# GpSimd makes the low part of every second half tile in the first stretch of the expert products

## The chip, the cores and the metric

The kernel runs on one core of a Trainium2 chip. The core has five engines that run side by side, each with its own queue of instructions taken in order: TensorE (PE in the profile, its weight loads PEld) multiplies matrices, VectorE (DVE) and ScalarE (ACT) work element by element, GpSimd (POOL) does element work too, and SyncE (SP) issues most transfers. [...] The metric is the device time of one execution in microseconds (us).

## The reference, cut to what matters

One decoder block for 256 tokens of width 2048: a projection, two kinds of attention, a gated merge, a layer norm, and then a retrieval over 16384 experts of one neuron each. The change lies in the last part, which reads, cut:

```python
def chunk(yc):                              # 128 tokens
    q = (yc @ w_q).reshape(PEER_CHUNK, PEER_HEADS, 2, half)
    s1 = einsum('chd,nd->chn', q[:, :, 0], sub_k1)
    s2 = einsum('chd,nd->chn', q[:, :, 1], sub_k2)
    v1, i1 = lax.top_k(s1, 16)
    v2, i2 = lax.top_k(s2, 16)
    ...
    sc, j = lax.top_k(cand, 16)             # of the sums v1 + v2
    eid = take_along_axis(cid, j, axis=-1)  # which experts
    gate = softmax(sc)
    act = gelu(einsum('chkd,cd->chk', u_tab[eid], yc))
    return einsum('chk,chkd->cd', gate * act, v_tab[eid])
```

The kernel multiplies the tokens with all rows of `u` and all rows of `v`, and brings in the choice of experts through tables of gates that are zero where an expert is not chosen.

## The kernel before, in words

Every float32 product is made of three passes in TensorE's float32r format. A weight tile `raw` is split into a high part `hi` (a cast) and a low part `lo = raw - hi`; the token matrix is split in the same way (`yhi`, `ylo`), and the passes are hi x yhi, lo x yhi and hi x ylo.

`Stream` (L56 to L130) does the splitting for all weights. A job is one weight tile of 128 x 1024 floats. `load_to` issues its transfer on SP's queue into one of three `raw` buffers; `split_upto` then treats the tile as two half tiles of 512 columns (b = 0 and b = 1): ScalarE makes `hi` of the half (L98), and VectorE makes `lo` of it (L99). There are six buffers each for `hi` and `lo`, so three tiles. The flag `share` sends `lo` of the half b = 1 to GpSimd in place of VectorE; it is set in a part of the attention and cleared later, and is off in the expert part.

`step` (L146) is the unit of the program. It takes the next split tile, runs what was deferred, takes at most one piece of background work from a list of `slots` when enough credit has gathered (each step gives a credit of 1, each piece has a cost), then calls `W.ahead()`, which writes the splits of the tiles up to two ahead into the queues, and last the matmuls of its own tile. So VectorE's and GpSimd's queues hold, for each step: the instructions of a background piece, if there is one, and behind them the `lo` of the tile that is used two steps later.

In the expert part, each of the 64 products `p` takes four steps of 24 matmuls (8 blocks of 128 x 128, three passes each), of which the second already needs `lo` of half 0 and the fifth `lo` of half 1. ScalarE applies GELU to the finished sum (L1251, `G<-acc`). While these products run, the background pieces choose the experts, in this order: `key_top` (the best 16 of 128 keys, 16 pieces of cost 1.7, on VectorE; half of them come before and half after a second batch of scores), and then for each of two tiles of 128 tokens t: `cands`, four `cand_top`, eight `pick` (cost 1.4), `gate` and `sel_T`. After those comes the piece that calls `open_G(1)` (it opens the second gate table and makes `keys` on GpSimd), and then 65 pieces that fill the gate tables.

A `pick` of head h is a small chain over two engines:

```python
V.tensor_tensor(eq, iota[...], posf[...], op=OP.is_equal)        # L1107, VectorE
GP.tensor_tensor(eq, eq, cid[...], op=OP.mult)                   # L1109, GpSimd
if (t, h - 1) in eqs:
    V.tensor_reduce(out=eid[:, t, h - 1, :], in_=eqs.pop((t, h - 1)), ...)   # L1111, VectorE
```

Before the expert part, `h_rows` (L1036, L1037) scales and shifts the normalised rows on GpSimd in 16 instructions of 128 x 512, and stores them.

Of the kernel before, what the change touches and what calls it, by code (L numbers as in the profile page):

```python
# [130 lines left out]
def block_kernel(ctx, tc, x, xT, w_in, rel_bias, onehot, lamq, lamk, subln_g, pe, w1, w2k, w2v, cmask,  # L131
# [11 lines left out]
    W = Stream(nc, stream, 3, 6)  # L143
# [40 lines left out]
    def bg(cost, pre, post=None):  # L184
        slots.append((cost, pre, post))
# [845 lines left out]
    def h_rows():  # L1031
        for t in range(2):
            for n in range(4):
                c = slice(n * 512, n * 512 + 512)
                d = r1[:, t, c]
                GP.tensor_tensor(d, d, gb[:, 0, c], op=OP.mult)  # L1036
                GP.tensor_tensor(d, d, gb[:, 1, c], op=OP.add)  # L1037
            GP.dma_start(h_d[:, t, :], r1[:, t, :])
# [112 lines left out]
    def open_G(i):  # L1151
        if i == 0:
            h_rows()
            pL.close()
        else:
            pT.close()
            gs["oh"] = pO.enter_context(tc.tile_pool(name="ohp", bufs=1, side="right"))
            gs["n0"] = len(stashed)
            keys = gs["keys"] = gs["oh"].tile([128, 128, 2], F16, name="keys")
            GP.iota(keys, pattern=[[1, 128], [0, 2]], base=0, channel_multiplier=0,  # L1160
                    allow_small_or_imprecise_dtypes=True)
        gp = pG[i].enter_context(tc.tile_pool(name=f"gp{i}", bufs=1))
        gs["G", i] = gp.tile([128, HI, S], F32, name=f"G{i}")
# [62 lines left out]
                pO.close()  # L1226
        deferred.append(ev)

    bg(0.1, lambda: open_G(1))
    for q in range(65):  # L1230
        bg(GCOST, lambda q=q: g_onehot(q) if q < 64 else None, lambda q=q: g_mm(q - 1) if q else None)

# [271 lines left out]
```

## Time and profile before

| | before |
|---|---|
| median of 3 runs | 2222.72 us (2221.65 to 2224.61) |
| the profiled execution | 2224.97 us |
| its span in the trace | 2223.2 us |
| PE busy | 2184.4 us, 98% |
| DVE busy | 1452.2 us, 65% |
| ACT busy | 1130.3 us, 51% |
| POOL busy | 246.5 us, 11% |

The time of the profiled execution is 1.8 us longer than its span, which runs from the first to the last instruction. Busy shares are averages over the whole span; the stretch that the change touches, from 765 to 970 us of the span, has other shares. TensorE's granted clock is full in all slices of it. A row of the trace gives where an instruction starts and how long it took; for an element engine an instruction that follows another on the same engine starts while the one before drains, so the distance between two starts (some 0.08 us less than the duration) is what a row of like instructions costs. An instruction that its engine has begun but that cannot get at its data shows as a longer duration and not as idle time.

### The profile page before, as it was taken

Reading aid. Unit: us, or ns where it says so; the run is one execution under the profiler, and the core shown is the slowest. Engines: PE = TensorE matmul, PEld = TensorE weight load, DVE = VectorE, ACT = ScalarE, POOL = GpSimd, SP = SyncE. Lnnn points to the kernel's source line nnn. Section 1 sums busy time; section 2 is a strip of 40 time slices with the busy share of each in tenths; the row PEclk is TensorE's granted clock in tenths of the full one; section 3 lists DMA queues with packets and bytes.
Section 4 is the critical chain, followed back from the end, with each engine's and each line's share of the span. In section 5 each row is a group of like instructions: output and inputs, shape, how many; then the busy total and the mean of one; then the engine's idle time right before and its main releaser. Section 6 shows DMA issues by size and latency. Waiting matters only on the chain.

```text
span 2223.2 us, 40705 instructions
## 1 busy us (share of the span) xinstructions
PE 2184.4 (98%) x15712; PEld 2016.0 (91%) x15712; DVE 1452.2 (65%) x2898; ACT 1130.3 (51%) x2153; POOL 246.5 (11%) x223
## 2 busy tenths in 40 slices
PE   9999999999999999999999999999999999999997
PEld 9988999999987999999999999998888888888786
DVE  5558774665767889988886555555555555555567
ACT  5555654665545444455554444445555455554443
POOL 2002234443001501210000000000000000000002
PEclk9999999999999999999999999999999999999999
DMA  7664564545675766555656666666666666667774
GB/s 243 195 186 155 173 198 130 166 151 162 202 226 160 238 183 189 181 185 181 182 183 190 196 194 194 193 197 206 196 191 194 193 193 196 192 197 236 253 220 143
DMA packets 119843, 424.72 MB, mean 191 GB/s; under 512 B 13876, under 2 KB 14212, under 8 KB 119392
## 3 DMA queue, kind: packets, MB, share of 16 engines
q1 hardware_dynamic: 111600, 398.90, 58.0%
q0 software_dynamic: 5600, 18.75, 2.8%
q10 hardware_dynamic: 2448, 4.46, 0.5%
q8 instruction: 123, 2.02, 0.4%
q14 instruction: 72, 0.59, 0.1%
HBM read 413.37 MB, written 8.69 MB: 190 GB/s over the span
## 4 chain that ended last, share of the span: by engine, by line
PE 75%; DVE 8%; DMA 5%; ACT 2%; issue 2%; POOL 1%; ACTq 0%; DVEq 0%; POOLq 0%; SPq 0%
PE acc L191 43%; PE o L191 27%; DVE lo L99 4%; PE lg L191 2%; DMA raw<-in_v_dram 2%; DMA raw<-in_w_in_dram 1%; PE pv L191 1%; DMA raw<-in_wout_dram 1%; DMA raw<-in_wq_dram 1%; ACT hi L98 1%; PE tp L539 1%; DVE eq L1107 0%; DVE eid L1111 0%; DVE st L901 0%; DVE r L933 0%
## 5 line engine op out<-in xcount | busy, mean ns | idle before, releaser
L99 DVE TENSOR_TENSOR lo<-raw,hi 128x512 fp32r<-128x512 f32 (+1 forms) x1422 | 980.8, 719 | 551.2 <-ACT hi L98 549.2
L98 ACT CAST hi<-raw 128x512 fp32r<-128x512 f32 (+1 forms) x1494 | 872.4, 617 | 692.5 <-PE o L191 267.6
L191 PE MATMUL acc<-yhi,lo 128*128 128x256 f32 x2112 | 586.7, 278 | 5.5 <-DVE lo L99 5.5
L191 PE MATMUL acc<-yhi,hi 128*128 128x256 f32 x2112 | 591.4, 280 | 0.0
L191 PE MATMUL acc<-ylo,hi 128*128 128x256 f32 x2112 | 584.1, 277 | 0.0
L191 PEld LDWEIGHTS acc<-yhi,lo 128*128 128x128 f32 x2112 | 397.0, 188 | 9.4 <-DVE lo L99 9.1
L191 PEld LDWEIGHTS acc<-yhi,hi 128*128 128x128 f32 x2112 | 396.8, 188 | 0.4 <-ACT hi L98 0.2
L191 PEld LDWEIGHTS acc<-ylo,hi 128*128 128x128 f32 x2112 | 396.7, 188 | 0.0
L191 PE MATMUL o<-lo,whi 128*128 128x512 f32 x1000 | 389.7, 390 | 0.8 <-DVE lo L99 0.8
L191 PE MATMUL o<-hi,whi 128*128 128x512 f32 x1000 | 389.4, 389 | 0.6 <-ACT hi L98 0.5
L191 PE MATMUL o<-hi,wlo 128*128 128x512 f32 x1000 | 389.1, 389 | 0.0
L191 PE MATMUL acc<-xhi,hi 128*128 128x256 f32 x1024 | 290.7, 284 | 4.2 <-ACT hi L98 4.2
L191 PE MATMUL acc<-xhi,lo 128*128 128x256 f32 x1024 | 286.5, 280 | 5.5 <-DVE lo L99 5.3
L191 PE MATMUL acc<-xlo,hi 128*128 128x256 f32 x1024 | 285.2, 279 | 0.0
L191 PEld LDWEIGHTS o<-lo,whi 128*128 128x128 f32 x1000 | 187.7, 188 | 42.0 <-DVE lo L99 3.1
L191 PEld LDWEIGHTS o<-hi,whi 128*128 128x128 f32 x1000 | 187.7, 188 | 40.9 <-ACT hi L98 1.5
L191 PEld LDWEIGHTS o<-hi,wlo 128*128 128x128 f32 x1000 | 187.7, 188 | 38.5
L191 PEld LDWEIGHTS acc<-xhi,lo 128*128 128x128 f32 x1024 | 194.1, 190 | 7.8 <-DVE lo L99 7.7
L191 PEld LDWEIGHTS acc<-xhi,hi 128*128 128x128 f32 x1024 | 194.4, 190 | 6.0 <-ACT hi L98 5.6
L191 PEld LDWEIGHTS acc<-xlo,hi 128*128 128x128 f32 x1024 | 193.9, 189 | 0.0
L1282 POOL DMA_DIRECT2D back<-act_d x17 | 9.3, 546 | 1170.5 <-DVE G L1290 607.4
L99 POOL TENSOR_TENSOR lo<-raw,hi 128x512 fp32r<-128x512 f32 x72 | 104.1, 1450 | 231.7 <-ACT hi L98 228.0
(308 smaller groups left out, 2170.3 us busy)
## 6 DMA issues: line engine op xcount, KB each, us to landing
raw<-in_u_dram SPq DMA_DIRECT2D x256, 512.0 KB, 4.1
raw<-in_v_dram SPq DMA_DIRECT2D x256, 512.0 KB, 3.6
raw<-in_w_in_dram SPq DMA_DIRECT2D x143, 512.0 KB, 4.1
raw<-in_wout_dram SPq DMA_DIRECT2D x32, 512.0 KB, 4.2
raw<-in_wbda_dram SPq DMA_DIRECT2D x16, 512.0 KB, 3.9
raw<-in_wbnsa_dram SPq DMA_DIRECT2D x16, 512.0 KB, 3.8
raw<-in_wq_dram SPq DMA_DIRECT2D x16, 512.0 KB, 4.2
raw<-in_w_in_dram SPq DMA_DIRECT2D x16, 280.0 KB, 3.0
```

Source lines behind the costliest of these rows:

```text
L98: self.nc.scalar.copy(hi[:, :w], r)
L99: (self.nc.gpsimd if self.share and b else sub).tensor_tensor(lo[:, :w], r, hi[:, :w].bitcast(F32), op=OP.subtract)
L191: PE.matmul(o, a, b, start=start, stop=stop, skip_group_check=True)
L539: PE.transpose(tp[:, 128 * b:128 * b + 128], P[:, 128 * b:128 * b + 128], ident)
L1282: GP.dma_start(t, act_d[vorder[n]])
```

## The change

`W.share` is set where the list of background pieces is written, just ahead of the first expert product, and cleared by the piece that opens the second gate table. Between the two, `lo` of the half b = 1 goes to GpSimd's queue.

```diff
+    def unshare():
+        W.share = False
+        open_G(1)
+
+    W.share = True
-    bg(0.1, lambda: open_G(1))
+    bg(0.1, unshare)
```

The instruction that moves is the one of L99, in `split_upto`:

```python
(self.nc.gpsimd if self.share and b else sub).tensor_tensor(lo[:, :w], r, hi[:, :w].bitcast(F32), op=OP.subtract)
```

On VectorE, at the picks of the first token tile (`eq<-iota,posf` is L1107 of a pick, `eid<-eq` the sum of the pick before it, `lo<-raw,hi` the low parts of one or two weight tiles):

```order
 L1107 TENSOR_TENSOR eq<-iota,posf 128x800
-L99 TENSOR_TENSOR lo<-raw,hi 128x512 x4
+L99 TENSOR_TENSOR lo<-raw,hi 128x512 x2
 L1107 TENSOR_TENSOR eq<-iota,posf 128x800
 L1111 TENSOR_REDUCE eid<-eq 128x16
-L99 TENSOR_TENSOR lo<-raw,hi 128x512 x2
+L99 TENSOR_TENSOR lo<-raw,hi 128x512
 L1107 TENSOR_TENSOR eq<-iota,posf 128x800
 L1111 TENSOR_REDUCE eid<-eq 128x16
-L99 TENSOR_TENSOR lo<-raw,hi 128x512 x4
+L99 TENSOR_TENSOR lo<-raw,hi 128x512 x2
 L1107 TENSOR_TENSOR eq<-iota,posf 128x800
```

Between two picks VectorE keeps one `lo` of each weight tile where it had two. Between the eight picks of a token tile lie 2, 1, 2, 1, 1, 2 and 1 weight tiles, so ten.

On GpSimd, from the store at the end of `h_rows` (`h_d<-r`) over the first picks (`eq<-eq,cid` is L1109):

```order
 L1038 DMA h_d<-r_8480 128x2048
-L1109 TENSOR_TENSOR eq<-eq,cid 128x800 x16
+L99 TENSOR_TENSOR lo<-raw,hi 128x512 x36
+L1109 TENSOR_TENSOR eq<-eq,cid 128x800
+L99 TENSOR_TENSOR lo<-raw,hi 128x512 x2
+L1109 TENSOR_TENSOR eq<-eq,cid 128x800
+L99 TENSOR_TENSOR lo<-raw,hi 128x512
+L1109 TENSOR_TENSOR eq<-eq,cid 128x800
```

GpSimd, which had only the 16 products of the picks in this stretch, has 71 low parts among them: 36 ahead of the first pick, 10 between the picks of each token tile, 11 between the two tiles, and 4 at the end, ahead of the making of `keys`. The queues of TensorE, ScalarE and SP keep their order.

## Rows read from the trace of the kernel before

**Rows 1.** The page: busy time of each engine, and VectorE in 40 slices.
```profile
PE 2184.4 (98%) x15712; PEld 2016.0 (91%) x15712; DVE 1452.2 (65%) x2898; ACT 1130.3 (51%) x2153; POOL 246.5 (11%) x223
...
DVE  5558774665767889988886555555555555555567
```

**Rows 2.** Busy time of each engine by stretch of the expert part.
```profile
core 0: us, PE busy (x) PEld busy (x) DVE busy (x) ACT busy (x) POOL busy (x), PEclk, DMA share, GB/s
770.00:865.00 95.00, 95.00 (x821) 94.39 (x821) 84.64 (x381) 46.06 (x81) 0.00 (x0) 1.00 0.64 194
865.00:900.00 35.00, 34.30 (x296) 33.60 (x294) 33.84 (x39) 15.17 (x28) 14.55 (x8) 1.00 0.55 174
...
1200.00:1500.00 300.00, 300.00 (x2650) 300.00 (x2649) 159.18 (x249) 139.09 (x249) 0.00 (x0) 1.00 0.65 194
```

**Rows 3.** Waits of PEld, 770 to 970 us: total us, times, longest.
```profile
PEld acc L191 <- DVE lo L99: 6.6, 15, 1.6
```

**Rows 4.** ScalarE in order of time, 855 to 870 us: start, duration, [idle before].
```profile
854.84 0.60 ACT L1251 ACTIVATE G<-acc 128x512 f32<-128x512 f32 x1 [1.92 <-PE acc L191]
...
865.72 0.60 ACT L1251 ACTIVATE G<-acc 128x512 f32<-128x512 f32 x1 [1.92 <-PE acc L191]
```

**Rows 5.** VectorE in order of time over the picks of the first token tile.
```profile
865.85 0.99 DVE L1107 TENSOR_TENSOR eq<-iota,posf 128x800 f32<-128x800 f32 x1
...
879.90 0.98 DVE L1107 TENSOR_TENSOR eq<-iota,posf 128x800 f32<-128x800 f32 x1
880.80 0.98 DVE L1111 TENSOR_REDUCE eid<-eq 128x16 f32<-128x800 f32 x1
881.70 2.24 DVE L99 TENSOR_TENSOR lo<-raw,hi 128x512 fp32r<-128x512 f32 x2
883.86 0.98 DVE L1107 TENSOR_TENSOR eq<-iota,posf 128x800 f32<-128x800 f32 x1
...
896.95 0.98 DVE L1107 TENSOR_TENSOR eq<-iota,posf 128x800 f32<-128x800 f32 x1
...
899.86 0.99 DVE L1115 TENSOR_REDUCE eid<-eq 128x16 f32<-128x800 f32 x1 [1.04 <-POOL eq L1109]
900.77 2.49 DVE L99 TENSOR_TENSOR lo<-raw,hi 128x512 fp32r<-128x512 f32 x4
```

**Rows 6.** GpSimd in order of time, 865 to 970 us.
```profile
881.03 1.76 POOL L1109 TENSOR_TENSOR eq<-eq,cid 128x800 f32<-128x800 f32 x1 [3.40 <-DVE eq L1107]
...
898.07 1.76 POOL L1109 TENSOR_TENSOR eq<-eq,cid 128x800 f32<-128x800 f32 x1 [2.19 <-DVE eq L1107]
```

**Rows 7.** GpSimd in order of time, `h_rows`.
```profile
739.79 1.74 POOL L1036 TENSOR_TENSOR r<-r,gd 128x512 f32<-128x512 f32 x1
...
743.19 1.74 POOL L1036 TENSOR_TENSOR r<-r,gd 128x512 f32<-128x512 f32 x1
...
746.59 1.73 POOL L1036 TENSOR_TENSOR r<-r,gd 128x512 f32<-128x512 f32 x1
```

**Rows 8.** VectorE in order of time, the same stretch.
```profile
738.95 13.83 DVE L99 TENSOR_TENSOR lo<-raw,hi 128x512 fp32r<-128x512 f32 x8 [1.22 <-ACT hi L98]
```

**Rows 9.** VectorE in order of time, 311 to 320 us (attention, `share` set).
```profile
311.74 2.36 DVE L630 TENSOR_TENSOR r<-r,gsub 128x1024 f32<-128x1024 f32 x1
...
318.65 1.23 DVE L630 TENSOR_TENSOR r<-r,gsub 128x1024 f32<-128x1024 f32 x1
```

**Rows 10.** GpSimd in order of time, 311 to 320 us.
```profile
311.72 1.29 POOL L99 TENSOR_TENSOR lo<-raw,hi 128x512 fp32r<-128x512 f32 x1 [1.09 <-DMA raw<-in_w_in_dram]
```

**Rows 11.** All `lo` on GpSimd: duration in ns, min/median/max.
```profile
L99 POOL TENSOR_TENSOR lo<-raw,hi x72: 1267/1358/1991, 298.1 to 701.9; 128x512 fp32r<-128x512 f32 x72
```

**Rows 12.** VectorE's groups, 770 to 865 us: busy us, mean ns, idle before.
```profile
L99 DVE TENSOR_TENSOR lo<-raw,hi 128x512 fp32r<-128x512 f32 x70 | 44.2, 685 | 10.3 <-ACT hi L98 10.3
```

## The prediction

> **What bounds the kernel now.** I read the page first. TensorE is busy 98% of the span, and VectorE 65%, but VectorE's slices are uneven: from the 14th to the 21st it stands at eight and nine tenths, against five in the last third [rows 1]. A slice is 55.6 us; the stretch of the change is the first half of that hump, so I cut it out. From 770 to 865 us, where the keys are ranked, VectorE is busy 84.64 of 95 us and TensorE the whole 95; from 865 to 900 us, the picks of the first token tile, VectorE is busy 33.84 of 35 and TensorE falls to 34.30; from 1200 to 1500 us TensorE is busy throughout beside a half idle VectorE [rows 2]. So TensorE sets the time nearly everywhere, and what it loses is lost at the end too, since nothing behind the stretch has idle time in which to win it back. The waits of the weight loads say how much there is: from 770 to 970 us they waited for `lo` 15 times, 6.6 us in all, 1.6 us at most [rows 3]. That is the most that a perfect version of this change could win, 0.3% of the time.
>
> The pace that TensorE wants comes from ScalarE's GELUs, one for every four steps: 865.72 - 854.84 = 10.88 us, so 2.72 us a step [rows 4]. At the picks the program asks for more than that. From the first `eq` to the eighth, 896.95 - 865.85 = 31.1 us pass [rows 5], and ten weight tiles are split in them, for which TensorE takes 27.2 us. VectorE is 3.9 us behind there; the tiles split ahead cover a part, and the rest, with the tail behind the eighth pick, are the waits of [rows 3].
>
> **Why VectorE is behind** decides this case. One cycle of a pick with one weight tile runs from 879.90 to 883.86 us, 3.96 us [rows 5]. By the starts of rows, `eq` costs 0.90 and the sum `eid` 0.90. The two `lo` should cost 0.60 each, as the four at 900.77 show (2.49 us: three distances of 0.60 and one duration of 0.69). But here the two take 2.24 us instead of 1.29: the first starts at 881.70, while GpSimd's product of the pick runs from 881.03 to 882.79 [rows 5, 6], and the pair ends 1.15 us behind that product's end, about the time of the two alone. So VectorE's subtraction stood still for 0.95 us until GpSimd was done. The sum `eid`, which reads one tensor, ran beside the same product at its usual 0.98 us. In `h_rows` the same is seen without a break: GpSimd starts an instruction of 128 x 512 twice per 3.40 us (739.79, 743.19, 746.59), so every 1.70 us [rows 7], and beside it eight `lo` take 13.83 us, 1.73 each in place of 0.60 [rows 8]. The two engines take turns. And where GpSimd made a `lo` in the attention part, VectorE's multiplication of two tensors took 2.36 us against 1.23 us a little later without it [rows 9, 10].
>
> [...]
>
> **The change, part by part.**
>
> 1. Removed from VectorE: 71 `lo` at 0.60 us, 43 us of its work. Where VectorE is not what TensorE waits for, this is worth nothing.
>
> 2. Added to GpSimd: the same 71. Alone one takes 1.27 us at the least and 1.36 us in the median [rows 11]. What matters is how long it keeps VectorE from its two-tensor instructions. A turn of both engines costs 1.70 us, of which 0.60 is VectorE's, so 1.10 us [rows 7, 8]; the multiplication that was held up gives 2.36 - 1.23 = 1.13 us [rows 9]. I take 1.10, from the stretch where the turns follow each other without a gap, as they will at the picks.
>
> 3. At the picks VectorE's queue alternates `eq`, `eid`, `lo`, and GpSimd's the product and `lo`. [...] Per weight tile 0.60 us go and 1.10 us come, +0.50 us. The cycle of 3.96 us becomes 4.46, where TensorE wants 2.72. Ten tiles between the first and the eighth pick: 31.1 + 5.0 = 36.1 us, against 27.2.
>
> 4. Two things are given back per token tile. Behind the eighth pick VectorE sums twice (the second from 899.86) and then splits (900.77) [rows 5]; GpSimd's `lo` can now run under the second sum. The second half of that weight tile then needs no 0.60 us behind the first, and GpSimd's turn costs a little of this: -0.4 us. And while keys are ranked, VectorE's other instructions read one tensor each, GpSimd's `lo` runs beside them, and the second half is ready earlier by up to one VectorE `lo`, 0.60 us; the splitting enters the picks with that much more lead: -0.5 us.
>
> 5. From 770 to 865 us VectorE made 70 `lo` in 44.2 us and idled 10.3 us before them [rows 12]; TensorE was busy for all 95 us there, and GpSimd idle [rows 2]. I cost the 35 that move at nothing: their cover is VectorE's idle time and the instructions with one input. What it costs if that cover fails is the third rival.
>
> 6. `W.share = True`, the piece `unshare` and the order on the other engines cost nothing: no instruction is added for them. The last four `lo` on GpSimd stand ahead of `keys`, some 5 us, where GpSimd sat idle in the trace before; if they were late, the first gate piece would start late with them.
>
> Sum: 5.0 - 0.4 - 0.5 = +4.1 us for each of the two token tiles, +8.2 us. On the profiled execution that makes 2224.97 + 8.2 = 2233.2 us; it stood 2.25 us above the median of its runs, so by the median 2222.72 + 8.2 = 2230.9, which I round to 2231.
>
> The bounds of the price: below, GpSimd always has a `lo` waiting and loses no time between VectorE's `eq` and its product (881.03 comes 0.23 us after VectorE's queue was free to go on, at 880.80), which saves seven times 0.23 = 1.6 us a tile, so +2.5 a tile and +5 in all. Above, each `lo` holds VectorE for its median of 1.36 us [rows 11]: +0.76 for ten tiles is 7.6, less 0.9, twice: +13.4 us. The forecast's own range is 2228 to 2236.
>
> **The rivals.**
>
> *Faster: the low parts of the two engines don't exclude each other.* Then the cycle loses 0.60 us a weight tile, 31.1 - 6.0 = 25.1 us, under TensorE's 27.2, and GpSimd's own queue (seven products of 1.76 and ten `lo` of 1.36, 25.9 us) just fits. All 6.6 us of waits would go: 2216 us. For it: the products at the picks are longer than a `lo` and read other tensors. Against it: [rows 7, 8] are a subtraction of just this kind beside a GpSimd instruction of the same size. It decides if a GpSimd `lo` holds VectorE under 0.60 us. 9%.
>
> *About the same.* The lead grows more than I allow, or GpSimd's `lo` falls under `eid` and under waits that exist now (the 0.95 us of [rows 5]), so that the picks cost 0 to 4.4 us in all: about 2225 us. [...] 15%.
>
> *Slower still: the ranking of keys falls behind too.* If every GpSimd `lo` holds VectorE for 1.10 us there as well, VectorE's 84.64 us become 84.64 + 35 x 0.50 = 102.1 us, over the 95 that TensorE gives [rows 2, 12]. The 7 us come in two waves, each covered in part by the lead; at worst all 7 are paid, and the picks begin without lead. +10 to +20 us, about 2238. For it: VectorE would have no idle time left. Against it: most of its work there reads one tensor. 14%.
>
> **The numbers.** Forecast 62% (+5 to +13.4), 14% slower still, 15% about the same, 9% faster. I call a difference under 0.2%, 4.4 us, no change, about what a measurement of this kernel can tell. Slower then has 0.62 + 0.14 = 0.76, same 0.15, faster 0.09. The range reaches to 2224 below, into the case of about the same, and to 2242 above, into the ranking case; it leaves out the faster case, a third of the same and the worst of the ranking, under 2 in 10.
>
> **What the new profile should show.** Between two picks with one weight tile some 4.5 us in place of 3.96, with two about 6.2. The waits of PEld for `lo` from 770 to 970 us grow from 6.6 to about 15 us, and a part of them names GpSimd. VectorE's `eq` rows are no longer 0.98 us but often 1.5 to 2, since they now wait for GpSimd's `lo`; GpSimd's `lo` are at 1.3 to 1.7 us. The ranking keeps TensorE busy without a gap. I am wrong if `eq` follows `eq` at less than 3.9 us, if VectorE's `lo` rows beside a GpSimd `lo` stay at 0.69 us, or if a new wait stands outside the picks, above all ScalarE's casts waiting longer for transfers because a `raw` buffer is now freed by the slower of two engines.

## The result, and the profile after

The changed kernel takes 2235.86 us in the median of 6 runs (2233.42 to 2239.81), the kernel before 2223.75 us in 6 runs on the same chip (2221.65 to 2224.76): a ratio of 1.0057, 95% interval 1.0047 to 1.0068. It is slower by about 12 us, where 8.2 were forecast; the time lies in the forecast range.

The profiled execution took 2235.15 us with a span of 2233.4, 10.2 more than before. The page, busy time and the slices of VectorE and GpSimd (answers [rows 1]):

```profile
PE 2186.7 (98%) x15712; PEld 2017.8 (90%) x15712; DVE 1448.1 (65%) x2827; ACT 1130.3 (51%) x2153; POOL 357.7 (16%) x294
...
DVE  5558774665667879988886555555555555555567
...
POOL 2002234442002646740000000000000000000002
```

71 instructions have left VectorE, and yet its busy time fell by 4 us only, since others became longer. Busy time by stretch, columns as in [rows 2]:

```profile
770.00:865.00 95.00, 95.00 (x824) 94.57 (x823) 74.45 (x342) 45.92 (x81) 47.94 (x35) 1.00 0.65 196
865.00:900.00 35.00, 31.84 (x266) 30.46 (x265) 34.50 (x24) 14.13 (x25) 28.34 (x17) 1.00 0.51 149
1200.00:1500.00 300.00, 300.00 (x2649) 300.00 (x2649) 159.87 (x250) 139.75 (x250) 0.00 (x0) 1.00 0.65 195
```

In the ranking VectorE is lighter by 10 us and TensorE full, as before. At the picks VectorE has 24 instructions in 35 us, is busy 34.50 us all the same, and TensorE gets through 266 matmuls where it had 296. Behind that the two kernels run alike (2650 and 2649 matmuls from 1200 to 1500 us). So the loss lies between the first GELU and the first `act`, two marks that enclose the stretch (before, then after; the tile view of `acc` on ScalarE, first and last start at the end):

```profile
L1255 ACT ACTIVATE act<-acc x47: 599/600/607, 973.0 to 1509.5; 128x512 f32<-128x512 f32 x47
L1251 ACT ACTIVATE G<-acc x17: 597/600/603, 776.3 to 959.4; 128x512 f32<-128x512 f32 x17
```

```profile
L1260 ACT ACTIVATE act<-acc x47: 599/599/608, 982.8 to 1519.9; 128x512 f32<-128x512 f32 x47
L1256 ACT ACTIVATE G<-acc x17: 597/598/603, 775.2 to 967.1; 128x512 f32<-128x512 f32 x17
```

973.0 - 776.3 = 196.7 us became 982.8 - 775.2 = 207.6: +10.9. I call this span from mark to mark *the stretch* below. Its first mark is not steady: from the first GELU to the second 9.55 us pass before and 10.03 after (776.30 to 785.85, 775.16 to 785.19), so 0.5 of the 10.9 us lie there, ahead of any wait of a weight load (the first one is at 887.96 before and at 878.71 after). The waits of PEld from 770 to 985 us, after (answers [rows 3]):

```profile
PEld acc L191 <- POOL lo L99: 9.0, 11, 1.3
PEld acc L191 <- DVE lo L99: 6.3, 6, 2.1
```

15.3 us in place of 6.6, and 9.0 of them name GpSimd; about 15, with a part on GpSimd, was forecast for 770 to 970 us, where there are 12.8 (the last wait, 2.15 us, and one of 0.34 come behind 970, since all is later by then). VectorE at the first `eq` of the first token tile, over one pick with one weight tile, and at the end of the tile, after (answers [rows 5]), and GpSimd beside the pick (answers [rows 6]):

```profile
864.70 0.99 DVE L1107 TENSOR_TENSOR eq<-iota,posf 128x800 f32<-128x800 f32 x1
...
880.26 2.07 DVE L1107 TENSOR_TENSOR eq<-iota,posf 128x800 f32<-128x800 f32 x1
882.25 0.97 DVE L1111 TENSOR_REDUCE eid<-eq 128x16 f32<-128x800 f32 x1
883.15 1.64 DVE L99 TENSOR_TENSOR lo<-raw,hi 128x512 fp32r<-128x512 f32 x1
884.71 2.07 DVE L1107 TENSOR_TENSOR eq<-iota,posf 128x800 f32<-128x800 f32 x1
...
899.73 2.07 DVE L1107 TENSOR_TENSOR eq<-iota,posf 128x800 f32<-128x800 f32 x1
...
903.74 0.98 DVE L1115 TENSOR_REDUCE eid<-eq 128x16 f32<-128x800 f32 x1 [1.04 <-POOL eq L1109]
```

```profile
882.47 1.76 POOL L1109 TENSOR_TENSOR eq<-eq,cid 128x800 f32<-128x800 f32 x1 [0.99 <-DVE eq L1107]
884.20 1.73 POOL L99 TENSOR_TENSOR lo<-raw,hi 128x512 fp32r<-128x512 f32 x1
886.92 1.76 POOL L1109 TENSOR_TENSOR eq<-eq,cid 128x800 f32<-128x800 f32 x1 [0.99 <-DVE eq L1107]
```

The cycle is 884.71 - 880.26 = 4.45 us; it was 3.96. VectorE's `lo` at 883.15 stands until the product has ended (884.23), and `eq` at 884.71 until GpSimd's `lo` has ended (885.93): 2.07 us in place of 0.98, so 1.09 us of standing still, at every pick of this token tile but the first. `eid`, with one input, is untouched (0.97 us, 0.98 before).

### The profile page after: what moved, and what is told of

It reads as the page before. It is cut to its first block, busy times and chain, and to the rows that moved or that the text cites. A ratio compares the mean times of both kernels' runs of the same rounds, so it can differ in the third digit from the quotient of the medians.

```text
span 2233.4 us, 40750 instructions
## 1 busy us (share of the span) xinstructions
PE 2186.7 (98%) x15712; PEld 2017.8 (90%) x15712; DVE 1448.1 (65%) x2827; ACT 1130.3 (51%) x2153; POOL 357.7 (16%) x294
## 3 DMA queue, kind: packets, MB, share of 16 engines
q10 hardware_dynamic: 2448, 4.46, 0.5%
q8 instruction: 123, 2.02, 0.4%
## 4 chain that ended last, share of the span: by engine, by line
PE 74%; DVE 7%; DMA 5%; issue 2%; ACT 2%; POOL 1%; ACTq 0%; POOLq 0%; DVEq 0%; SPq 0%
PE acc L191 43%; PE o L191 27%; DVE lo L99 3%; PE lg L191 2%; DMA raw<-in_v_dram 2%; PE pv L191 1%; DMA raw<-in_wout_dram 1%; DMA raw<-in_u_dram 1%; DMA raw<-in_wq_dram 1%; ACT hi L98 1%; POOL lo L99 1%; POOL eq L1109 1%; DVE eq L1107 1%; PE tp L539 1%; DVE st L901 0%
## 5 line engine op out<-in xcount | busy, mean ns | idle before, releaser
L99 DVE TENSOR_TENSOR lo<-raw,hi 128x512 fp32r<-128x512 f32 (+1 forms) x1351 | 952.2, 731 | 566.2 <-ACT hi L98 564.5
L99 POOL TENSOR_TENSOR lo<-raw,hi 128x512 fp32r<-128x512 f32 x143 | 213.8, 1500 | 294.1 <-ACT hi L98 284.7
```

Of the source, the lines that this page charges most:

```text
L99: (self.nc.gpsimd if self.share and b else sub).tensor_tensor(lo[:, :w], r, hi[:, :w].bitcast(F32), op=OP.subtract)
```

## The experiments

Twelve kernels, each compared with the kernel before on its own chip. All compute the whole reference; the three with dummies add work that nobody reads.

| kernel | median us | before | ratio (95%) | stretch us |
|---|---|---|---|---|
| e_rank_only | 2221.60 | 2222.74 | 0.9997 (0.9988-1.0006) | 196.8 |
| e_pick_only | 2228.18 | 2222.74 | 1.0026 (1.0017-1.0036) | 202.0 |
| e_pool_reads | 2250.13 | 2222.74 | 1.0122 (1.0106-1.0137) | 223.9 |
| e_pool_writes | 2262.08 | 2222.74 | 1.0182 (1.0167-1.0198) | 201.6 |
| e_pool_writes2 | 2222.01 | 2222.71 | 0.9995 (0.9986-1.0005) | 196.4 |
| e_prod_dve | 2231.28 | 2222.21 | 1.0042 (1.0029-1.0056) | 205.9 |
| e_prod_dve_noshare | 2221.21 | 2222.21 | 0.9996 (0.9987-1.0005) | 195.8 |
| e_pick2 | 2214.03 | 2222.21 | 0.9964 (0.9950-0.9977) | 223.2 * |
| e_after_pick2 | 2224.90 | 2222.21 | 1.0009 (0.9999-1.0018) | 232.4 * |
| e_not_between | 2228.75 | 2222.71 | 1.0026 (1.0017-1.0035) | 206.0 |
| e_between_only | 2226.91 | 2222.71 | 1.0014 (1.0005-1.0023) | 198.0 |
| e_gate1_off | 2231.63 | 2223.57 | 1.0039 (1.0025-1.0052) | 205.3 |

\* three more products lie ahead of the first `act` there (20 `G<-acc` and not 17), so only these two compare with each other.

**Half of the change: the ranking alone.** `share` is set as in the change and cleared by the first `cands`.

```diff
+    W.share = True
     for p in range(NP):
+    def cands_off(t):
+        W.share = False
+        cands(t)
```

> The low parts of the second halves go to GpSimd only while the keys are ranked; at the picks VectorE makes all again. Turns at the port (my theory): the ranking costs nothing and the picks are as before, so -1.5 to +1 us against the kernel before, about 2223 us, and the cycle of a pick with one tile is back at 3.96 us. Rival, that each low part on GpSimd costs wherever it stands (later freed buffers, a slower engine): 35 of 71 stay, so about half of the 12 us, some 2229 us.

No loss: the low parts that GpSimd makes beside the ranking (29 here, up to 840.3 us) cost nothing that can be measured, and the lead that they might give wins nothing measurable either. The third rival (the ranking falls behind) is out.

**The other half: the picks alone.** `share` on in each pick piece, off in the gate pieces.

```diff
-            bg(1.4, lambda t=t, h=h: pick(t, h))
-        bg(1.5, lambda t=t: gate(t))
+            bg(1.4, lambda t=t, h=h: sharing(True, lambda: pick(t, h)))
+        bg(1.5, lambda t=t: sharing(False, lambda: gate(t)))
```

> The low parts of the second halves go to GpSimd only from the first pick to the gate of each token tile; while keys are ranked VectorE makes all. Turns at the port: the whole loss stays, +10 to +13 us against the kernel before, 2233 to 2237 us, cycles of 4.45 and 6.15 us. If the loss came from the ranking, 2225 us or less.

A miss: the picks lose, but 5.4 us, about half of what the whole change loses. VectorE and GpSimd in this kernel show why the cycles are shorter than in the changed one:

```profile
879.50 0.89 DVE L99 TENSOR_TENSOR lo<-raw,hi 128x512 fp32r<-128x512 f32 x1
880.30 2.55 DVE L1107 TENSOR_TENSOR eq<-iota,posf 128x800 f32<-128x800 f32 x1
882.78 0.97 DVE L1111 TENSOR_REDUCE eid<-eq 128x16 f32<-128x800 f32 x1
883.68 0.87 DVE L99 TENSOR_TENSOR lo<-raw,hi 128x512 fp32r<-128x512 f32 x1
884.47 2.54 DVE L1107 TENSOR_TENSOR eq<-iota,posf 128x800 f32<-128x800 f32 x1
```

```profile
879.79 2.22 POOL L1109 TENSOR_TENSOR eq<-eq,cid 128x800 f32<-128x800 f32 x1
881.97 2.03 POOL L99 TENSOR_TENSOR lo<-raw,hi 128x512 fp32r<-128x512 f32 x1
883.96 2.20 POOL L1109 TENSOR_TENSOR eq<-eq,cid 128x800 f32<-128x800 f32 x1
```

The turns come in another order. The product runs late, beside the *next* `eq`; GpSimd has no idle time; and its `lo`, once `eq` is done at 882.85, lies mostly under `eid`. This cycle takes 884.47 - 880.30 = 4.17 us (one-tile cycles behind a two-tile one take 3.68 to 3.70, two-tile ones some 6.3), and from the first `eq` to the last sum each token tile takes 37.1 us: +3.1 and not +5.0. In the changed kernel the first token tile runs in the one order (39.0 us) and the second mostly in the other (37.0; 34.0 before). That was not foreseen.

**Why do they exclude each other?** Two dummies beside the kernel before, from the first product until the second gate table is opened: GpSimd reads one half tile with every `hi` of b = 1, or it only writes.

```diff
+        GP.tensor_tensor(junk, hi.bitcast(F32), hi.bitcast(F32), op=OP.subtract)   # e_pool_reads
...
+        A.copy(tick, junk[i % 3][:, 0:1])                                          # e_pool_writes
+        GP.iota(junk[i % 3], pattern=[[1, 256]], ...)
...
+        for _ in range(3):                                                         # e_pool_writes2
+            GP.iota(part, pattern=[[1, 240]], ...)
```

> The kernel before, VectorE makes all low parts, and GpSimd makes beside them, where the change put a low part, a subtraction of hi from itself into a scratch tile that nobody reads. Turns at the port: every such instruction takes its 1.1 us of turn with nothing given back, so a pick with one tile takes 3.96 + 1.10 = 5.06 us, ten tiles cost 11 us a token tile, +22 us for the picks and up to 10 more if the ranking falls behind too: 2245 to 2256 us. Rival, that the loss of the change is the wait for a slower engine's result behind the product in its queue: nobody waits for these, so no change, 2222 to 2225 us.

> As the kernel with the added subtractions, but the added GpSimd instruction only writes (an iota of 256 float16 that took 1.51 us in the trace of before), and ScalarE reads one element of its old content first, which sets its pace. If the turns are for reading SBUF: within 3 us of the kernel before, 2222 to 2226 us, and VectorE's low parts beside it stay at 0.69 us. If any GpSimd instruction takes a turn: 2245 us or more.

> The added write-only instructions again, three iotas of 240 float16 a weight tile (about 0.33 us each), in a scratch of 1024 bytes a partition, the size that left TensorE's pace as it was in the kernel with the added subtractions; the 1540 bytes of the first attempt slowed every product of the rest by 3%. If the turns are for reading SBUF: within 3 us of the kernel before, 2220 to 2226 us. If GpSimd's writing takes turns too: 2235 us or more.

Reading cost 27 us, as this theory wanted, though not all by the price that it named: a pick with one tile takes 4.74 us and not 5.06, and two spells of half clock (0.83 granted from 910 to 920 and from 950 to 960 us) are in its profile. The first writing kernel misled: its time is far above before, but not through the picks (from 764 to 1000 us its weight loads waited 4.0 us, before 6.6). With its scratch tiles (some 1540 bytes in each partition) TensorE was slower in the expert part and behind it (2144 matmuls from 1600 to 2100 us, 2192 before); its window from 1220 to 1480 us, where the dummy had long ended, holds 2210 matmuls against 2296 in the kernel before, each in 260 busy us at full clock:

```profile
1220.00:1480.00 260.00, 260.00 (x2210) 260.00 (x2210) 133.01 (x208) 116.14 (x208) 0.00 (x0) 1.00 0.61 187
```

So its time says nothing on the turns. The second writing kernel, with 1024 bytes of scratch and with three writes per tile that keep GpSimd busy for 1.13 us, nearly as long as a `lo`, does. VectorE and GpSimd there:

```profile
883.16 2.18 DVE L100 TENSOR_TENSOR lo<-raw,hi 128x512 fp32r<-128x512 f32 x2
885.27 0.98 DVE L1110 TENSOR_TENSOR eq<-iota,posf 128x800 f32<-128x800 f32 x1
```

```profile
882.43 1.77 POOL L1112 TENSOR_TENSOR eq<-eq,cid 128x800 f32<-128x800 f32 x1 [1.06 <-DVE eq L1110]
884.15 1.13 POOL L1239 IOTA junk<- 128x240 f16 x3
```

VectorE's two `lo` wait for the product (it ends at 884.20) and then run beside the writes at their old pace, 2.18 us in all where the kernel before has 2.24; the `eq` behind them stays at 0.98 us, the cycle takes 3.89 us, and the time is that of before. So GpSimd's reading is what takes the turn in these runs: `eq` takes 2.07 us beside a GpSimd `lo` in the changed kernel, and two `lo` take 2.18 us, no longer than before, beside the writes. "The port" in the expectations is my name for whatever it is that the two engines take in turn; the runs show the turns, and not what stands behind them.

**Is it the product's place in GpSimd's queue?** A rival to the turns: the product waits behind a `lo`. The product goes to VectorE, with and without the change.

```diff
-        GP.tensor_tensor(eq, eq, cid[:, t, h, None, :]..., op=OP.mult)
+        V.tensor_tensor(eq, eq, cid[:, t, h, None, :]..., op=OP.mult)
```

> The changed kernel with the product of a pick on VectorE, so that GpSimd has nothing but low parts. Turns at the port: a pick's product costs 0.9 us of turn in place of 1.76, a low part on GpSimd still 1.1 of which the sum of the pick can hide up to 0.9: ten tiles and seven picks take 30 to 34 us, where the changed kernel takes 35.0 and TensorE wants 27.2, so 2220 to 2230 us. Rival, the low part's place behind the product in GpSimd's queue is what hurts, not the turn: then all of the loss goes, 2217 us or less.

> The kernel before with the product of a pick on VectorE: nothing of it is on GpSimd any more. VectorE alone then needs 7 x 2.7 + 20 x 0.6 = 30.9 us from the first to the eighth pick, where the kernel before takes 31.1: no difference, 2221 to 2224 us. It says whether GpSimd was of any use at the picks.

Without sharing the move is free (0.99 us more on VectorE a pick, where GpSimd's product held its `lo` for 0.95 us before; GpSimd is idle there now). With sharing it loses 10 us against that, though GpSimd now has nothing but `lo`; the 2231.28 us lie just above the 2220 to 2230 expected. The tile view of `eq` in e_prod_dve, ns min/median/max:

```profile
L1109 DVE TENSOR_TENSOR eq<-eq,cid x16: 991/1964/2123, 862.5 to 961.5; 128x800 f32<-128x800 f32 x16
```

The product itself is now what stands still, for 1.0 us. So it is not the queue.

**Is it the density of the picks?** A pick gets a cost of 2.0 credits instead of 1.4, so that more weight tiles, and more of TensorE's time, lie between two picks; in the kernel before and in the changed one.

```diff
-            bg(1.4, lambda t=t, h=h: pick(t, h))
+            bg(2.0, lambda t=t, h=h: pick(t, h))
```

> The kernel before with a pick's cost raised from 1.4 to 2.0, so that two weight tiles lie between any two picks. Turns at the port: a pick with two tiles takes 5.16 us in the trace of before, less than the 5.44 us of two steps, so TensorE's 6.6 us of waits at the picks go and nothing comes for them: 2216 to 2218 us. Rival, that the waits come from the tail of the picks and from the gates alone: 2 to 4 us of them stay, 2219 to 2222 us.

> The changed kernel with the same cost of 2.0. A pick with two tiles takes 6.15 us there, against 5.44: 0.7 us behind per pick, 5 us in seven, of which the tiles split ahead cover some 2.5: waits of 2 to 4 us a token tile, so near the kernel before, 2220 to 2225 us, and 4 to 8 us above the kernel with cost 2.0 and no sharing. If the slower engine's result as such were the trouble, one more step between picks would not help: 2230 us or more.

The first is the fastest kernel of the study, 8 us under the kernel before and under the 2216 to 2218 expected: it removes the waits that the change was to remove, 6.4 of 6.6 us; what the rest of its gain is was not looked into. From 764 to 1000 us one is left:

```profile
PEld acc L191 <- DVE lo L99: 0.2, 1, 0.2
```

With the change on top, 10.9 us come back, more than the 4 to 8 expected: two tiles lie between most picks now, their two GpSimd `lo` add 1.0 us to a cycle of 5.2, and 6.1 to 6.2 us again exceed the 5.44 that TensorE needs for two. So density decides whether VectorE is late, and the turns keep their price.

**Where is the rest?** The two halves alone add up to some 5 us, not 12. Three kernels take the pieces between and behind the picks apart: e_not_between has no sharing from each gate piece to the next tile's first pick, e_between_only has it only there (and ahead of the first picks and at the second gate), e_gate1_off ends it at the second token tile's gate, one piece earlier than the change, which returned three `lo` to VectorE (68 are left on GpSimd of 71).

```diff
+        bg(2.5, lambda t=t: sharing(False, lambda: cands(t)))                      # e_not_between
+            bg(1.4, lambda t=t, h=h: sharing(True, lambda: pick(t, h)))
+        bg(1.5, lambda t=t: sharing(False, lambda: gate(t)))
...
+        bg(2.5, lambda t=t: sharing(True, lambda: cands(t)))                       # e_between_only
+            bg(1.4, lambda t=t, h=h: sharing(False, lambda: pick(t, h)))
+        bg(1.5, lambda t=t: sharing(True, lambda: gate(t)))
...
+    def last_gate():                                                               # e_gate1_off
+        W.share = False
+        gate(1)
+        bg(1.5, lambda t=t: last_gate() if t else gate(t))
```

> The changed kernel with sharing off in the pieces between (from the gate of a token tile to the first pick of the next, and ahead of the first pick): 29 low parts stay on GpSimd in the ranking and 12 to 13 at the picks of each token tile. If the change's loss is the picks (5.4 us, as sharing there alone measured) and a lead used up between them (the other half), this falls to 2227 to 2229 us, as with sharing at the picks alone. If the ranking takes lead from the picks, it stays at 2231 us or more.

> Sharing only in the pieces between: 7 low parts on GpSimd ahead of the first picks, 9 between the token tiles, 3 behind the last. If they cost VectorE time by themselves (its casts and two-input instructions of cands, gate and the best-16 search standing still for GpSimd), +4 to +6 us, 2226 to 2229 us. If they only hurt because the picks before them have used up the lead, 0 to +2 us, 2222 to 2225 us.

> The changed kernel, with the sharing ended one piece earlier: at the gate piece of the second token tile instead of the piece that opens the second gate table. Four of the 71 low parts go back to VectorE, the last ones. In the changed kernel's profile the cast and the scalar_tensor_tensor of that piece took 1.20 and 1.25 us instead of 0.23 and 0.29, the weight load behind them waited 2.15 us, and the granted clock was 0.83 in the 10 us after it. Theory (the part of the loss that the forecast did not have is this gate piece: 1.2 us of waits and 1.7 us of half clock): both operations are back at 0.23 and 0.29 us, the waits of PEld from 966 to 985 us fall from 2.5 to about 1.3 us, the clock stays at 1.00 there, the stretch from the first GELU to the first act falls from 207.6 to about 204.7 us, the median is 2231.5 to 2234. Rival 1 (the drop of the clock belongs to the pile of waits at the picks, not to the one behind the gate): the operations are short again, the clock still falls once in the stretch, 206 to 207 us, median 2234 to 2236. Rival 2 (the missing time is lost between the two token tiles): nothing moves, 207 to 208 us, 2235 to 2237.

The first came out as expected, +6.0 (its profiled execution was its slowest, 2231.78 us, with 1.7 us of half clock in it). The second can't tell its two theories apart: by the medians, +4.2, it falls in the range of the first (2226 to 2229), but its stretch is only 1.3 us longer than before, as the second had it, and its profiled execution was its slowest, with the other 3.2 us of its +4.5 outside the stretch (1.5 of them in the v products, 700.0 us that became 701.5); it shows the place (a new wait of 2.44 us behind the second gate piece), not the price. The third shows most. First the changed kernel: VectorE at the second gate piece, GpSimd, the weight load behind it, and the granted clock (third number from the right) from 970 to 980 and from 976 to 979 us:

```profile
971.88 1.20 DVE L1128 CAST sel<-eidi 128x128 f32<-128x128 int32 x1
973.11 1.25 DVE L1129 SCALAR_TENSOR_TENSOR sel<-sel,eid 128x128 f32<-128x128 f32 x1
974.29 2.97 DVE L99 TENSOR_TENSOR lo<-raw,hi 128x512 fp32r<-128x512 f32 x3
```

```profile
971.67 2.54 POOL L99 TENSOR_TENSOR lo<-raw,hi 128x512 fp32r<-128x512 f32 x2 [2.21 <-ACT hi L98]
```

```profile
975.02 0.19 PEld L191 LDWEIGHTS acc<-yhi,lo 128*128 128x128 f32 x1 [2.15 <-DVE lo L99]
```

```profile
970.00:980.00 10.00, 7.98 (x53) 7.78 (x54) 6.71 (x12) 3.62 (x8) 3.88 (x4) 0.83 0.52 154
976.00:979.00 3.00, 3.00 (x16) 3.00 (x16) 1.26 (x2) 0.00 (x0) 0.11 (x1) 0.50 0.81 206
```

Two small operations of 0.23 and 0.29 us stand still for 1.0 us each beside GpSimd's two `lo`. VectorE's next `lo` is late by that, TensorE waits 2.15 us, and then the granted clock falls to 0.50 for some 3.4 us. By the row of 10 us that costs (1.00 - 0.83) x 10 = 1.7 us. Now e_gate1_off, at the same place, with the waits of PEld from 966 to 985 us at the end:

```profile
973.71 0.23 DVE L1128 CAST sel<-eidi 128x128 f32<-128x128 int32 x1
973.97 0.29 DVE L1129 SCALAR_TENSOR_TENSOR sel<-sel,eid 128x128 f32<-128x128 f32 x1
974.18 3.69 DVE L99 TENSOR_TENSOR lo<-raw,hi 128x512 fp32r<-128x512 f32 x6
```

```profile
970.00:980.00 10.00, 9.86 (x81) 9.28 (x80) 7.54 (x17) 5.91 (x12) 2.65 (x3) 1.00 0.64 201
```

```profile
PEld acc L191 <- POOL lo L99: 1.1, 1, 1.1
PEld acc L191 <- DVE lo L99: 0.7, 3, 0.3
```

The operations are short again, the clock stays full, and behind the gate 0.7 us of waits are left of 2.5, where 1.3 were expected (the 1.1 is one wait at 966.37 that belongs to the picks; it lies just ahead of the window in the changed kernel). With the 1.7 us of clock that makes 3.5, of which the stretch shows 2.3: it is 205.3 us in place of 207.6, and not the 204.7 expected, for a wait of 0.92 us that the changed kernel does not have stands at the first token tile's gate piece (at 913.43 us). The kernel takes 2231.63 us, 8.1 over the kernel before. Its interval (1.0025 to 1.0052) touches that of the change, and the two did not run side by side, so it is the traces that count. That the wait comes with the sharing is shown by more than these two: e_between_only, which shares at this gate, has it, and e_pick_only and e_not_between, which don't, have none above 0.33 us there. That the drop of the clock belongs to it is likely, with one trace of each kernel, and not shown.

## Why the prediction was right, point by point

**The place and the mechanism** were right: TensorE waits at the picks, VectorE and GpSimd take turns, and +0.50 us per weight tile comes in. The one-tile cycle was forecast at 4.46 us and is 4.45; the two-tile cycle at about 6.2 and is 6.15 (880.26 - 874.11). From the end of the first `eq` to the end of the eighth the first token tile takes 36.1 us, as part 3 had it (from start to start only 35.0, since the eighth `eq` stands still behind its start), and by the waits it loses 7.1 - 3.3 = 3.8 us against the 4.1 of the sum. GpSimd's hold of 1.10 us was measured at 1.09, and not at the 1.27 that a `lo` takes alone. That every weight tile pays the whole +0.50 us of part 3 no run shows: the first token tile paid it, and in the other order of turns, where GpSimd's `lo` lies mostly under `eid`, a token tile pays 3.0 or 3.1 us of the 5.0.

**The ranking** (part 5) costs nothing that can be measured, as shown by e_rank_only. **The faster rival** would have needed `lo` to pass each other; [rows 7, 8] were the right rows, and the writing dummy shows which half of GpSimd's work takes the turn. The wait that the prediction named as its own danger, ScalarE's casts waiting longer for transfers, did grow (33.0 to 55.5 us from 764 to 985 us), but no weight load waited there before the picks or between them: its waits lie from 878.71 to 905.53 and from 940.35 to 975.02 us, where VectorE was late in the picks or the gate. Another sign that it named, a new wait outside the picks, did come: the 2.15 us behind the second gate piece.

**What the sum left out** is larger than what it mis-sized. The waits, cut at 906 and 966 us after (905 and 959 before), add up so: first token tile 3.3 to 7.1, second tile's picks 2.0 to 5.6, second gate 1.3 to 2.5, together +8.6; the half clock adds 1.7. That makes 10.3 of the stretch's 10.9, and 0.5 lie between the first two GELUs, where no weight load waits. The picks lost 7.4 us where the sum has 8.2, and 2.9 us came on top that it does not have. So the mechanism was right, and that the total lies inside the range is in part luck: the upper bound, +13.4, was worked out from a longer hold of GpSimd's `lo`, and not from the gate or the clock. Three things:

- The gate piece was costed at nothing beside GpSimd's last `lo` (part 6). It costs 1.2 us of waits here (1.8 against e_gate1_off): its SCALAR_TENSOR_TENSOR has two inputs, and part 4's rule, that VectorE's instructions with one input run freely, does not hold for its cast (0.23 us that became 1.20).
- The sum has no term for the clock. The six executions of the changed kernel had mean granted clocks of 0.993 (2239.81 us) to 0.996 (2233.42 and the profiled one). More drops in the slower ones would fit the median's +12.1 against the profile's +10.2, but that is not shown: only one execution was traced, and the mean takes in drops anywhere. The clock was full in the slices of the page only; both kernels' traces have half clock near 12 us (0.83 granted from 10 to 20 us) and near 350 us (0.89 to 0.94 in the two rows of 10 us there), far from the change.
- The second token tile's picks ran in the other order of turns and lengthened by 3.0 us and not 5.0, but lost 3.6 us all the same, near the 4.1 of the sum by luck. The tail behind the eighth pick was given back about as forecast in the first tile (its last waiting weight load starts 905.53 - 903.74 = 1.79 us behind the last sum; before it was 902.10 - 899.86 = 2.24); the 0.5 us of lead per tile was not seen in the time of any run.

What stays open is what chooses between the two orders of turns. The changed kernel runs its first tile in one and its second mostly in the other, e_pick_only both in the faster, e_after_pick2 both in the slower; no run forced it.

## What to carry to other kernels

Before moving an element operation to GpSimd, ask whether it reads SBUF and whether VectorE's work beside it has two inputs or is a cast: here the move of a 0.60 us subtraction cost 1.09 us of the engine that it was meant to relieve. It was free where VectorE ranked (MAX8 of L1065 on 128x128 took 0.278 us in the median from 770 to 930 us, 0.285 before), and dear where it compared and multiplied. And before moving work off a late engine, look whether it is late only because its work is bunched: a cost of 2.0 for a pick took away all but 0.2 us of the waits and won 8 us.

## What the runs showed of the hardware that I had not expected

- VectorE's small conversions stand still for a GpSimd `lo` though they read one tensor: CAST 0.23 to 1.20 us, TENSOR_SCALAR (L1082) 0.23 to 1.28, while TENSOR_REDUCE beside the same work stays at 0.97.
- The same pieces on two queues fell into two orders of turns: a pick with one tile takes 4.45 us in one, and 3.68 to 4.17 us in the other.
- The granted clock fell to 0.50 after a wait of 2.15 us, but not after one of 2.02 us in the same kernel or of 2.44 us in e_between_only. From 764 to 1000 us it fell in e_prod_dve and e_not_between once and in e_pool_reads twice, each time for some 3.4 us at or just behind a wait of a weight load (2.03 us in e_not_between, 3.44 in e_prod_dve, 1.03 twice in e_pool_reads).
- With some 1540 bytes of scratch per partition TensorE got through 3.7% fewer matmuls (2210 against 2296 in 260 us at full clock), with 1024 bytes through as many as before (2297). Why stays open.
